# A hybrid GLA and attention trunk on one core: output-pair weight sums held behind low parts, products with g_post deferred, and loads moved ahead in the last pair

## The chip, the cores and the metric

The kernel runs on one NeuronCore of a Trainium2 chip. The metric is the device time of one execution in microseconds (us); lower is better. TensorE (PE) does the matrix products, with its weight loads shown as PEld; VectorE (DVE) and ScalarE (ACT) do elementwise work; GpSimd (POOL) issues some of the DMAs and does small powers; SyncE (SP) issues most DMAs. Each engine takes its instructions in the order of its own queue.

## The reference, cut to what matters

Two layers, 512 tokens, width 2048, float32. `w_in` has 7184 columns per layer, `w_out` 2048.

```python
def rmsnorm(x, g):
    y = xf * lax.rsqrt(jnp.mean(xf * xf, axis=-1, keepdims=True) + EPS) * g
def hybrid_layer(x, w_in, w_out, g_pre, g_post, ...):
    h = rmsnorm(x, g_pre)
    z = h @ w_in
    ...                       # gated linear attention, chunked attention, gates
    y = jnp.concatenate([o_gla, o_att], axis=-1) @ w_out
    return x + rmsnorm(y, g_post)
```

The change lies in the output projection `y = ... @ w_out`, its norm with `g_post` and the residual sum.

## The kernel before, in words

**Products.** Each float32 product is made of three matmuls in a rounded format (fp32r): the weight is split into a high part `wh` (a cast on ScalarE, L195) and a low part `wl` (source less high part, on VectorE, L203), the other operand likewise, and high·high, high·low and low·high are added up in PSUM. `w` lies in blocks of 512 columns, cut in 8 chunks of 256 rows; a chunk of one block is a tile of 128x1024 (512 KB).

**Jobs.** All weight tiles of the whole program form one list, `stream`, of objects `Job`. A job has three steps. `load` issues its DMAs on SP; `high` makes the sum or difference of weights that it needs (L189, L191 on VectorE) and then the cast; `low` makes the low part. The function `ahead` prepares, while job i is multiplied, loads up to five, `high` up to four and `low` up to three jobs in front. A job is 12 matmuls of 128x512.

**Two kinds of product.** `std_gemm` multiplies block by block. `fast_gemm` multiplies a pair of blocks as a 2x2 block product with seven products instead of eight (Winograd's form of Strassen): the kinds are P1 to P7, each with four chunks c, so 28 jobs. P5, P6 and (in the output pairs) P4 add a freshly loaded weight tile `r` to the running tile `H`; P7 takes a difference. The order of a pair is written out: `PROD_OUT` for the first output pair (W01), `PROD_END` for the second (W23) of the last layer:

```python
PROD_END = order("10 20 11 21 12 22 13 23 50 51 60 52 61 53 62 63 30 31 32 33 70 71 72 73 40 41 42 43")
PROD_OUT = order("10 20 11 21 12 13 50 51 60 61 22 23 52 53 62 63 30 31 32 33 70 71 72 73 40 41 42 43")
```

("51" is P5 with c = 1.) W23 of the first layer goes through `std_gemm`.

**Operands of the output pairs.** P1, P2 and P4 use the operands themselves (`og`, `op_att`: tiles `a` and `g`); P5, P6, P3 and P7 use their sums S1, S2, S4, S3. `output_sums` makes these during W01 on VectorE (L1157, then the low part L106) and ScalarE, each queued behind the latest low part of a weight. In the last layer they also go to DRAM (`so_d`, tile `oS`), and W23 loads them back as `sa`, a ring of four tiles.

**Rings.** `H` has four tiles, `raw` five, `wh` four, `wl` three, `sa` four; a load waits on SP until a tile of its ring is free.

**After a product.** `finished` hands each half result to `project`: its square sum on ScalarE (L1301), then the product with `g_post` on VectorE (L1304) into `ys`. Where the result is still to be combined (`combine`, L341), it goes to a scratch tile `t2` first. `finish_token` later scales with the norm and adds the residual. In W23 of the last layer the residual of the last 256 tokens is loaded by `Tokens.load` (L452), one or two of its six pieces after each job of P7; P7's own weight tiles are loaded into spare slots `g` at P3's load.

**Order.** The program text only gives dependencies and priorities: a planner puts each engine's instructions in an order by a simulated timeline. `tc.issue_after(x)` adds one edge: what is traced inside it stands behind x in its engine's queue, not necessarily right behind it. Side work runs as generators in `tasks`, stepped by `pump` from a `Pace` of so many steps per job.

Of the kernel before, what the change touches and what calls it, by code (L numbers as in the profile page):

```python
# [15 lines left out]
P = 128  # L16
# [17 lines left out]
def hybrid_trunk(  # L34
# [30 lines left out]
    def nm(s):  # L65
        serial[0] += 1
        return f"{s}_{serial[0]}"
# [65 lines left out]
    PROD_OUT = order("10 20 11 21 12 13 50 51 60 61 22 23 52 53 62 63 30 31 32 33 70 71 72 73 40 41 42 43")  # L133
    LEFT = {"P5": "S1", "P6": "S2", "P3": "S4", "P7": "S3", "P4": "A22"}
    SPARE = ("g12", "g13", "g16", "g17")
    last_cast, last_low, last_mm, last_load = [None], [None], [None], [None]

    class Job:
        def __init__(self, l, kind, c, b0, b1=None, pair=None):
# [13 lines left out]
        def load(self):  # L153
            k, c, p, b0, b1 = self.kind, self.c, self.pair, self.b0, self.b1
            end = b0 >= NB_IN and k != "std"
            if end:
                c = OC[c]
            top, bottom = (c + 4, c) if end else (c, c + 4)
            if k == "std":
                self.raw = self.fetch(rtile("raw", bufs=5), b0, c)  # L160
            elif k == "P1":
                p["H", self.c] = self.fetch(rtile("H"), b0, top)
            elif k == "P5":
                p["r", self.c] = self.fetch(rtile("raw", bufs=5), b1, top)
            elif k == "P6":
                p["r", self.c] = self.fetch(rtile("raw", bufs=5), b1, bottom)
            elif k == "P7":
                p["r", self.c] = p.pop(("t", self.c)) if b0 == W23[0] else self.fetch(rtile("raw", bufs=5), b0, top)
            elif k == "P2" or (k == "P4" and end):
                p["r", self.c] = self.fetch(rtile("raw", bufs=5), b0, bottom)  # L170
            sums = so_d if end else sa_d[self.l]
            src = sums.get((LEFT.get(k), c))
            if src is not None and b0 != NB_IN and not (k == "P5" and b0 == AV0):
                until(lambda: k == "P4" or (id(sums), LEFT[k], c) in written)
                self.a = rtile("sa", (2, 512), F32R)
                last_load[0] = nc.sync.dma_start(flat(self.a), src).ins
            if k == "P3" and b0 == W23[0]:
                with tc.issue_after(last_load[0]):
                    p["t", self.c] = self.fetch(slot(SPARE[self.c], [2, 512]), b0, c + 4)

        def high(self):
            k, c, p = self.kind, self.c, self.pair
            if k == "std":
                src = self.raw
            else:
                h, r = p["H", c], p.get(("r", c))
                src = h if k in ("P1", "P5", "P6", "P4") else r
                if k in ("P5", "P6") or (k == "P4" and self.b0 >= NB_IN):
                    nc.vector.tensor_tensor(out=h, in0=h, in1=r, op=ALU.add)  # L189
                elif k == "P7":  # L190
                    nc.vector.tensor_tensor(out=r, in0=h, in1=r, op=ALU.subtract)  # L191
            self.src = src
            self.wh = rtile("wh", dtype=F32R)
            for z in self.parts():
                last_cast[0] = nc.scalar.copy(self.wh[:, z, :], src[:, z, :]).ins  # L195
# [4 lines left out]
        def low(self):  # L200
            self.wl = rtile("wl", dtype=F32R, bufs=3)
            for z in self.parts():
                last_low[0] = nc.vector.tensor_tensor(  # L203
                    out=self.wl[:, z, :], in0=self.src[:, z, :], in1=self.wh[:, z, :].bitcast(F32), op=ALU.subtract
                ).ins
            if self.kind == "P2" and self.b0 < NB_IN:
                h = self.pair["H", self.c]
                nc.vector.tensor_tensor(out=h, in0=h, in1=self.src, op=ALU.add)  # L208
# [237 lines left out]
    XS1 = ("g9", "g10")  # L446

    class Tokens(list):
        def load(self, n=None):
            for z, src in self.moves[:n]:  # L450
                with tc.issue_after(last_load[0]):
                    nc.sync.dma_start(z, src)  # L452
            del self.moves[:n]

# [249 lines left out]
    def layer(l):  # L704
# [476 lines left out]
        def turn_gla(h, p):  # L1181
            ps = aux()
            for f in range(2):
                for tt in range(2):
                    nc.tensor.transpose(
                        ps[:, f * 256 + tt * P : f * 256 + (tt + 1) * P],
                        normed[h, p][:, tt, f * P : (f + 1) * P], ident,
                    )
            assert p or h >= 2 or ("P2", h) in passed
            op = slot(OG[p, h], [2, 512], F32R)  # L1190
            full_o = out_parts(h)[2 * p + 1]
            for f in range(2):
# [8 lines left out]
            if len(og) == 8:  # L1201
                for n in range(2):
                    gains.append(tmp.tile([P, W], F32, tag="bias", name=nm("bias"), bufs=2))
                    load_gain(n, gains[n])

        def gla_heads(j, gvh, gvl):
            units = []
# [83 lines left out]
            nc.sync.dma_start(gp, bass.AP(tensor=src.tensor, offset=src.offset, ap=[[0, P], [1, W]]))  # L1291
            return gp

        def project(o, n, src, gp, between=None):
            if o not in ssy:
                ssy[o] = sm(5, "ssy", 4)
                nc.gpsimd.memset(ssy[o][:, 4:5], EPS)
            if (o, n // 2) not in ys:
                ys[o, n // 2] = slot(YS[n // 2][o], [1024])
            j = t2(dtype=BF16)  # L1300
            nc.scalar.activation(j, src, AF.Square, scale=D ** -0.5, accum_out=ssy[o][:, n : n + 1])  # L1301
            if between is not None:
                between()
            nc.vector.tensor_tensor(  # L1304
                out=ys[o, n // 2][:, (n % 2) * W : (n % 2 + 1) * W], in0=src, in1=gp, op=ALU.mult
            )

        def out_evac(n):
            gp = load_gain(n, t2())
# [42 lines left out]
        def out_consume(n):  # L1352
            if n:
                gains[:] = [load_gain(n + j, t2()) for j in range(2)]
            ends = []

            def f(j, h, t, src, comb):
                until(lambda: len(gains) == 2)
                o = 2 * h + t
                ending = last and n == 2 and (j, h) == (0, 1)  # L1360

                def begin():
                    ends.append(finish_token(o, xs[1][t]))
                    next(ends[-1])

                with nullcontext() if n and (j, h) == (0, 1) else tc.issue_after(last_low[0]):
                    project(o, n + j, src if comb is None else comb(t2()), gains[j], begin if ending else None)
# [12 lines left out]
        drain()  # L1380

        def residual(k, c):
            if (k, c) == ("P3", 3):
                xs[1] = load_tokens(1, x_src)
            elif k == "P7":
                xs[1].load(2 if c > 1 else 1)

        if last:
            fast_gemm(
                l, W23, out_consume(2), rate=3, end=True, lag=2, ops=O,  # L1390
                after=residual,
            )
        else:
            for half in range(2):
                for b in W23:
                    if b == W23[1]:
                        xs[half] = load_tokens(half, x_src)
                        xs[half].load()
# [65 lines left out]
```

## Time and profile before

| | |
|---|---|
| median of 3 runs | 1643.17 us (1640.9 to 1645.68) |
| the profiled execution's own time | 1639.9 us |
| its span in the profile | 1637.8 us |
| mean granted TensorE clock | 0.997 |
| TensorE busy | 1613.9 us (99%) |
| VectorE busy | 1253.2 us (77%) |
| ScalarE busy | 911.4 us (56%) |
| HBM read, written | 371.25 MB, 55.33 MB |

Times in the rows of the trace count from the start of the span. In a timeline a row gives the start, the duration, engine, line, operation, `out<-in` by the program's names, shapes and count; in brackets stand the idle time of the engine before it and what ended it. A window row gives, behind the stretch and its length, the busy time of PE, PEld, DVE, ACT and POOL with the number of instructions, then the granted TensorE clock, the busy share of the DMA engines and GB/s. The matmuls are pipelined, so the duration of one (about 0.39 us) is longer than the distance from start to start.

### The profile page before, as it was taken

What the parts mean: (1) busy time and instruction counts of PE and PEld (TensorE: products, weight loads), DVE (VectorE), ACT (ScalarE), POOL (GpSimd) and SP (SyncE); (2) the same over time, 40 slices, a digit from 0 to 9 for tenths busy, and PEclk for the clock granted to TensorE, in tenths of its full rate; (3) what the DMA queues carried; (4) which work ended last, traced back from release to release, by engine and by line L of the source; (5) the groups of instructions that cost most, each with busy time, mean ns of one, the idle gap of its engine ahead of it and who ended that gap; (6) DMA issues with size and microseconds to landing.
All of it is one profiled execution on the core that took longest, in us unless ns stands there. A gap on an engine that the chain in (4) does not pass through costs nothing.

```text
span 1637.8 us, 24501 instructions
## 1 busy us (share of the span) xinstructions
PE 1613.9 (99%) x8986; PEld 1382.4 (84%) x8986; DVE 1253.2 (77%) x1630; ACT 911.4 (56%) x1497; POOL 122.0 (7%) x182
## 2 busy tenths in 40 slices
PE   9999999999999999999999999999999999999996
PEld 7888999998888778788788889999988887787885
DVE  5987778687787868995786667776776878699976
ACT  7554445666554556654674444455665545566553
POOL 0120000100000100000122000000000101101001
PEclk9999999999999999999999999999999999999999
DMA  9698685785869667277989486858858596785967
GB/s 368 239 377 283 229 308 196 251 305 173 297 201 354 223 220 262 95 262 267 332 278 398 172 309 220 305 184 271 272 175 296 186 333 232 232 297 200 347 232 228
DMA packets 130759, 426.10 MB, mean 260 GB/s; under 512 B 14052, under 2 KB 26852, under 8 KB 130608
## 3 DMA queue, kind: packets, MB, share of 16 engines
q1 hardware_dynamic: 115632, 370.22, 65.2%
q0 software_dynamic: 14432, 53.24, 8.8%
q8 instruction: 71, 1.16, 0.3%
q10 hardware_dynamic: 576, 1.08, 0.2%
q14 instruction: 48, 0.39, 0.1%
HBM read 371.25 MB, written 55.33 MB: 260 GB/s over the span
## 4 chain that ended last, share of the span: by engine, by line
PE 89%; DVE 5%; DMA 4%; issue 1%; ACT 1%; DVEq 0%; POOL 0%; SPq 0%; ACTq 0%; POOLq 0%
PE mm L384 46%; PE mm L374 19%; PE mm L306 12%; PE ax L907 2%; DVE wl L203 1%; PE ax L384 1%; PE ax L1092 1%; DMA H<-in_w_dram 1%; PE ax L890 1%; DMA raw<-in_w_dram 1%; DMA x_mid<-g 1%; PE ax L1064 1%; DVE g L106 1%; PE ax L871 1%; PE ax L870 1%
## 5 line engine op out<-in xcount | busy, mean ns | idle before, releaser
L384 PE MATMUL mm<-wh,sa 128*128 128x512 f32 x1472 | 479.1, 395 | 6.4 <-DMA sa<-oS 4.8
L195 ACT CAST wh<-raw 128x1024 fp32r<-128x1024 f32 (+1 forms) x249 | 261.3, 1053 | 223.1 <-PE mm L384 88.1
L203 DVE TENSOR_TENSOR wl<-raw,wh 128x1024 fp32r<-128x1024 f32 (+1 forms) x249 | 302.5, 1218 | 92.2 <-PE mm L384 31.6
L195 ACT CAST wh<-H 128x1024 fp32r<-128x1024 f32 x240 | 251.6, 1051 | 212.2 <-PE mm L384 96.8
L203 DVE TENSOR_TENSOR wl<-H,wh 128x1024 fp32r<-128x1024 f32 x240 | 292.9, 1222 | 91.8 <-PE mm L384 34.4
L384 PEld LDWEIGHTS mm<-wh,sa 128*128 128x128 f32 x1472 | 276.5, 188 | 74.1 <-issue 11.7
L384 PE MATMUL mm<-wl,sa 128*128 128x512 f32 x736 | 288.9, 392 | 4.3 <-DVE wl L203 4.3
L374 PE MATMUL mm<-sa,wh 128*128 128x256 f32 x1280 | 236.8, 285 | 0.0
L384 PE MATMUL mm<-wh,a 128*128 128x512 f32 x608 | 200.5, 394 | 0.5 <-ACT wh L195 0.5
L374 PEld LDWEIGHTS mm<-sa,wh 128*128 128x128 f32 x1280 | 200.0, 191 | 0.3
L374 PE MATMUL mm<-sa,wl 128*128 128x256 f32 x640 | 181.1, 283 | 0.0
L189 DVE TENSOR_TENSOR H<-H,raw 128x1024 f32<-128x1024 f32 x132 | 160.3, 1221 | 7.9 <-DMA raw<-in_w_dram 6.6
L384 PEld LDWEIGHTS mm<-wl,sa 128*128 128x128 f32 x736 | 138.7, 188 | 32.5 <-DVE wl L203 5.4
L384 PEld LDWEIGHTS mm<-wh,a 128*128 128x128 f32 x608 | 113.5, 188 | 24.4 <-ACT wh L195 0.9
L374 PEld LDWEIGHTS mm<-sa,wl 128*128 128x128 f32 x640 | 122.5, 191 | 0.0
L425 POOL TENSOR_TENSOR sm<-sm,mhalf 128x2 f32<-128x2 f32 (+2 forms) x42 | 52.8, 1258 | 934.3 <-DVE sm L917 452.5
L384 PE MATMUL mm<-wl,a 128*128 128x512 f32 x304 | 119.8, 394 | 0.0
L191 DVE TENSOR_TENSOR raw<-H,raw 128x1024 f32<-128x1024 f32 x56 | 68.6, 1225 | 45.2 <-DMA raw<-in_w_dram 45.0
L374 PE MATMUL mm<-a,wh 128*128 128x256 f32 x512 | 95.3, 285 | 0.0
L306 PE MATMUL mm<-wh,a 128*128 128x512 f32 x288 | 91.5, 390 | 0.0
L384 PE MATMUL mm<-wh,g 128*128 128x512 f32 x288 | 90.9, 390 | 0.2 <-ACT wh L195 0.2
L208 DVE TENSOR_TENSOR H<-H,raw 128x1024 f32<-128x1024 f32 x48 | 58.7, 1224 | 33.2 <-DMA raw<-in_w_dram 33.2
(235 smaller groups left out, 2429.3 us busy)
## 6 DMA issues: line engine op xcount, KB each, us to landing
raw<-in_w_dram SPq DMA_DIRECT2D x319, 512.0 KB, 4.9
sa<-S SPq DMA_DIRECT2D x184, 512.0 KB, 4.4
H<-in_w_dram SPq DMA_DIRECT2D x60, 512.0 KB, 5.1
sa<-A SPq DMA_DIRECT2D x48, 512.0 KB, 6.1
S<-g POOLq DMA_DIRECT2D x32, 512.0 KB, 8.9
sa<-oS SPq DMA_DIRECT2D x16, 512.0 KB, 5.9
oa<-g POOLq DMA_DIRECT2D x12, 512.0 KB, 6.4
g<-in_x_dram SPq DMA_DIRECT2D x10, 512.0 KB, 9.1
```

Of the source, the lines that this page charges most:

```text
L106: return nc.vector.tensor_tensor(out=lo, in0=src, in1=hi.bitcast(F32), op=ALU.subtract).ins
L189: nc.vector.tensor_tensor(out=h, in0=h, in1=r, op=ALU.add)
L191: nc.vector.tensor_tensor(out=r, in0=h, in1=r, op=ALU.subtract)
L195: last_cast[0] = nc.scalar.copy(self.wh[:, z, :], src[:, z, :]).ins
L203: last_low[0] = nc.vector.tensor_tensor(out=self.wl[:, z, :], in0=self.src[:, z, :], in1=self.wh[:, z, :].bitcast(F32), op=ALU.subtract).ins
L208: nc.vector.tensor_tensor(out=h, in0=h, in1=self.src, op=ALU.add)
L306: nc.tensor.matmul(pss[o], a(part, kk, o) if callable(a) else a[:, part, t], rhs[:, kk, :], start=(i == 0 and kk == 0 and m == 0), stop=(i ...
L374: nc.tensor.matmul(dst, lhs[:, kk, f], a[:, part, tok], start=(fresh and kk == 0 and m == 0 and ft % 2 == 0), stop=(c == 3 and kk == 1 and ...
L384: last_mm[0] = nc.tensor.matmul(out_ps[t], a[:, part, tok], rhs[:, kk, :], start=(fresh and kk == 0 and m == 0), stop=(c == 3 and kk == 1 ...
L425: nc.gpsimd.tensor_tensor(out=out_r, in0=v, in1=mhalf[:, : v.shape[-1]], op=ALU.pow)
L870: nc.tensor.matmul(ps[:, :n], self.qh[:, t], self.kl[:, :n], start=False, stop=False)
L907: nc.tensor.matmul(o, self.pt[i][:, j * P : (j + 1) * P], av[hd // 4, j // 2][:, j % 2, (hd % 4) * P : (hd % 4 + 1) * P], start=(j == 0), ...
```

## The change

Three edits. In the output pairs, `high` traces its addition or subtraction of weights inside `issue_after(lows[-2])`, where `lows` lists the low parts of all jobs. W01's results are no longer multiplied with `g_post` where they are evicted: `project` leaves the plain result in `ys`, and a generator `late_gains` multiplies the eight halves in place during W23. In W23 of the last layer the residual's six pieces are loaded one at a time behind `last_h`, the load of P1's last `H`, and P7's weight tiles are fetched at P5's load, also behind it.

```diff
+    lows = []
...
             elif k == "P1":
                 p["H", self.c] = self.fetch(rtile("H"), b0, top)
+                last_h[0] = last_load[0]
...
-            if k == "P3" and b0 == W23[0]:
-                with tc.issue_after(last_load[0]):
+            if k == "P5" and b0 == W23[0]:
+                with tc.issue_after(last_h[0]):
                     p["t", self.c] = self.fetch(slot(SPARE[self.c], [2, 512]), b0, c + 4)
...
-                if k in ("P5", "P6") or (k == "P4" and self.b0 >= NB_IN):
-                    nc.vector.tensor_tensor(out=h, in0=h, in1=r, op=ALU.add)
-                elif k == "P7":
-                    nc.vector.tensor_tensor(out=r, in0=h, in1=r, op=ALU.subtract)
+                with tc.issue_after(lows[-2]) if self.b0 >= NB_IN else nullcontext():
+                    if k in ("P5", "P6") or (k == "P4" and self.b0 >= NB_IN):
+                        nc.vector.tensor_tensor(out=h, in0=h, in1=r, op=ALU.add)
+                    elif k == "P7":
+                        nc.vector.tensor_tensor(out=r, in0=h, in1=r, op=ALU.subtract)
...
+            lows.append(last_low[0])
...
-        def project(o, n, src, gp, between=None):
+        def project(o, n, src, gp=None, comb=None, between=None):
...
+            dst = ys[o, n // 2][:, (n % 2) * W : (n % 2 + 1) * W]
+            y = src if comb is None else comb(dst if gp is None else t2())
+            if gp is None and comb is None:
+                nc.scalar.copy(dst, src)
...
-            nc.vector.tensor_tensor(
-                out=ys[o, n // 2][:, (n % 2) * W : (n % 2 + 1) * W], in0=src, in1=gp, op=ALU.mult
-            )
+            if gp is not None:
+                nc.vector.tensor_tensor(out=dst, in0=y, in1=gp, op=ALU.mult)
+
+        def late_gains():
+            gs = [load_gain(n, t2()) for n in range(2)]
+            for o in range(NT):
+                for n in range(2):
+                    for _ in range(3):
+                        yield
+                    dst = ys[o, 0][:, n * W : (n + 1) * W]
+                    with tc.issue_after(last_low[0]):
+                        nc.vector.tensor_tensor(out=dst, in0=dst, in1=gs[n], op=ALU.mult)
...
         drain()
+        tasks.append(late_gains())
 
         def residual(k, c):
-            if (k, c) == ("P3", 3):
+            if (k, c) == ("P2", 0):
                 xs[1] = load_tokens(1, x_src)
-            elif k == "P7":
-                xs[1].load(2 if c > 1 else 1)
+            if k in ("P1", "P2") and xs:
+                xs[1].load(last_h[0], 1)
```

More of the change, by code (lines that the diff above doesn't have):

```diff
@@ L135, in hybrid_trunk @@
     SPARE = ("g12", "g13", "g16", "g17")
-    last_cast, last_low, last_mm, last_load = [None], [None], [None], [None]
+    lows = []
+    last_cast, last_low, last_mm, last_load, last_h = [None], [None], [None], [None], [None]
     class Job:
@@ L448, in hybrid_trunk, with load @@
     class Tokens(list):
-        def load(self, n=None):
+        def load(self, behind, n=None):
             for z, src in self.moves[:n]:
-                with tc.issue_after(last_load[0]):
+                with tc.issue_after(behind):
                     nc.sync.dma_start(z, src)
@@ L1200, in turn_gla @@
             O[1, p, OC.index(h)] = op
[L1201 to L1204, printed above, removed]
         def gla_heads(j, gvh, gvl):
@@ L1299, in project @@
                 ys[o, n // 2] = slot(YS[n // 2][o], [1024])
+            dst = ys[o, n // 2][:, (n % 2) * W : (n % 2 + 1) * W]
+            y = src if comb is None else comb(dst if gp is None else t2())
+            if gp is None and comb is None:
+                nc.scalar.copy(dst, src)
             j = t2(dtype=BF16)
-            nc.scalar.activation(j, src, AF.Square, scale=D ** -0.5, accum_out=ssy[o][:, n : n + 1])
+            nc.scalar.activation(j, y, AF.Square, scale=D ** -0.5, accum_out=ssy[o][:, n : n + 1])
             if between is not None:
                 between()
-            nc.vector.tensor_tensor(
-                out=ys[o, n // 2][:, (n % 2) * W : (n % 2 + 1) * W], in0=src, in1=gp, op=ALU.mult
-            )
+            if gp is not None:
[9 more added lines that the diff above has]
+                        nc.vector.tensor_tensor(out=dst, in0=dst, in1=gs[n], op=ALU.mult)
         def out_evac(n):
@@ L1357, in f @@
             def f(j, h, t, src, comb):
-                until(lambda: len(gains) == 2)
                 o = 2 * h + t
@@ L1366, in f @@
                 with nullcontext() if n and (j, h) == (0, 1) else tc.issue_after(last_low[0]):
-                    project(o, n + j, src if comb is None else comb(t2()), gains[j], begin if ending else None)
+                    project(o, n + j, src, gains[j] if n else None, comb, begin if ending else None)
                 if last and n == 2 and (j, h, t) == (1, 0, 1):
@@ L1397, in layer @@
                         xs[half] = load_tokens(half, x_src)
-                        xs[half].load()
+                        xs[half].load(last_load[0])
                     std_gemm(l, b, (2 * half, 2 * half + 1), OL, operand_out, out_evac(b - NB_IN), rate=3, lag=2)
```

## The prediction

> **What bounds the kernel now.** I began with the page's engine totals.
>
> ```profile
> span 1637.8 us, 24501 instructions
> PE 1613.9 (99%) x8986; PEld 1382.4 (84%) x8986; DVE 1253.2 (77%) x1630; ACT 911.4 (56%) x1497; POOL 122.0 (7%) x182
> ```
>
> TensorE sets the time: 1613.9 of 1637.8 us busy. The diff touches no matmul, so it can gain only what TensorE idles, or runs at a lower clock, in the output pairs (W01 of both layers, W23 of the last). I therefore took a table of windows over the span and went into those where PE falls short.
>
> ```profile
> core 0: us, PE busy (x) PEld busy (x) DVE busy (x) ACT busy (x) POOL busy (x), PEclk, DMA share, GB/s
> 688.00:692.00 4.00, 1.95 (x7) 1.35 (x8) 4.00 (x5) 3.79 (x6) 0.00 (x0) 1.00 0.00 0
> 1508.00:1510.00 2.00, 2.00 (x6) 1.60 (x5) 2.00 (x3) 2.00 (x5) 0.00 (x0) 0.50 0.21 84
> 1510.00:1512.00 2.00, 2.00 (x8) 1.56 (x7) 2.00 (x4) 1.45 (x4) 0.00 (x0) 0.73 0.00 0
> 1565.00:1570.00 5.00, 5.00 (x24) 4.14 (x23) 4.22 (x4) 3.04 (x4) 0.00 (x0) 1.00 0.35 107
> 1600.00:1605.00 5.00, 3.00 (x12) 2.18 (x12) 2.06 (x3) 0.26 (x1) 0.00 (x0) 1.00 1.04 400
> ```
>
> There are three holes: W01 of layer 0 (about 690) and of layer 1 (before 1508, seen by the clock of 0.50 behind it), both with VectorE full, and W23 of layer 1 (1600) with the DMA engines full, although 35 us earlier, at 1565, they were busy for 0.35 only. The timeline of PE gives their sizes.
>
> ```profile
> 686.69 0.39 PE L384 MATMUL mm<-wh,sa 128*128 128x512 f32 x1
> 688.44 0.73 PE L384 MATMUL mm<-wh,sa 128*128 128x512 f32 x2 [1.36 <-ACT wh L195]
> 690.78 0.50 PE L384 MATMUL mm<-wl,sa 128*128 128x512 f32 x1 [1.61 <-DVE wl L203]
> 1503.11 0.40 PE L384 MATMUL mm<-wh,sa 128*128 128x512 f32 x1
> 1503.80 0.73 PE L384 MATMUL mm<-wh,sa 128*128 128x512 f32 x2 [0.30 <-ACT wh L195]
> 1507.26 0.50 PE L384 MATMUL mm<-wl,sa 128*128 128x512 f32 x1 [2.72 <-DVE wl L203]
> 1598.07 0.39 PE L384 MATMUL mm<-wh,sa 128*128 128x512 f32 x1
> 1601.66 0.47 PE L384 MATMUL mm<-wh,sa 128*128 128x512 f32 x1 [3.20 <-DMA sa<-oS]
> 1604.05 0.39 PE L384 MATMUL mm<-wl,sa 128*128 128x512 f32 x1
> 1604.27 0.39 PE L384 MATMUL mm<-wh,sa 128*128 128x512 f32 x1
> 1606.25 0.47 PE L384 MATMUL mm<-wh,sa 128*128 128x512 f32 x1 [1.59 <-DMA sa<-oS]
> ```
>
> Matmuls in step start 0.22 to 0.23 us apart (1604.05, 1604.27), so a job of 12 takes 2.7 us, and a hole is the next start less the last start less 0.23 per matmul. Layer 0: 688.44 − 686.92 = 1.52 and 690.78 − 688.90 = 1.88, together **3.40 us**. Layer 1: 0.46 + 3.00 = **3.46 us**. W23: 3.36 + 1.75 = **5.11 us**. Behind the layer-1 hole the granted clock halves: 2.0 us at 0.50 and 2.0 us at 0.73, which lose 1.0 and 0.5, **1.5 us**. All that can be won is 3.40 + 3.46 + 1.5 + 5.11 = 13.5 us, 0.8% of the time.
>
> **The change part by part.** *(a) VectorE's order in the output pairs.* Each add or subtract of weights (L189, L191) is now held behind the low part (L203) of the job two in front. What stood ahead of the late low parts (689.50 and 1505.97, both of P6's third job):
>
> ```profile
> 661.51 1.23 DVE L189 TENSOR_TENSOR H<-H,raw 128x1024 f32<-128x1024 f32 x1 [2.52 <-DMA raw<-in_w_dram]
> 662.65 1.22 DVE L203 TENSOR_TENSOR wl<-H,wh 128x1024 fp32r<-128x1024 f32 x1
> 684.29 1.22 DVE L191 TENSOR_TENSOR raw<-H,raw 128x1024 f32<-128x1024 f32 x1
> 685.43 0.69 DVE L106 TENSOR_TENSOR sa<-t,sa 128x512 fp32r<-128x512 f32 x1
> 689.50 1.23 DVE L203 TENSOR_TENSOR wl<-H,wh 128x1024 fp32r<-128x1024 f32 x1
> 1479.24 2.36 DVE L189 TENSOR_TENSOR H<-H,raw 128x1024 f32<-128x1024 f32 x2 [2.44 <-DMA raw<-in_w_dram]
> 1502.50 1.23 DVE L191 TENSOR_TENSOR raw<-H,raw 128x1024 f32<-128x1024 f32 x1
> 1505.97 1.23 DVE L203 TENSOR_TENSOR wl<-H,wh 128x1024 fp32r<-128x1024 f32 x1
> L195 ACT CAST wh<-H 128x1024 fp32r<-128x1024 f32 x240 | 251.6, 1051 | 212.2 <-PE mm L384 96.8
> ```
>
> An instruction of 128x1024 holds the queue for 685.43 − 684.29 = 1.14 us. L191 at 684.29 (1502.50) is P7's first subtract, six jobs ahead of its turn: P6's third job is the 15th of the pair, P7's first the 21st. Held behind the low part of the 19th, it leaves the way: 1.14 us in each layer. The add at 661.51 is P6's first; it made VectorE idle 2.52 us for its load while a ready low part (662.65, P5's first) stood behind it. Now that low part goes ahead and fills 1.14 us of the idle time; layer 1 has the same picture at 1479.24 (2.44 us). So 2 × 1.14 = **2.3 us** of each hole goes, and 1.1 us stays. Bounds: nothing (the planner orders other work into the place) to the whole 3.40 and 3.46. I take 2.3, the two named rows. With a hole of 1.1 us I let the clock's 1.5 us go as well, because layer 0's holes of 1.52 and 1.88 us left the clock at 1.00 (688 to 692). Sum of (a): 2.3 + 2.3 + 1.5 = **6.1 us**, bounds 0 and 8.4. The hold puts an add behind a low part two jobs in front, which leaves it two jobs, 5.4 us, for add (1.2), cast (1.1, the L195 row) and low (1.2): nobody waits for that unless the low part itself is late.
>
> The Trainium skill, TensorE: Matmul & The Clock Gate, Part 1, says that the clock drops to half after an idle window of about 3.4 us, and that the window runs freely. Here a hole of 3.00 us (3.46 with the two matmuls in it) was followed by half speed and one of 3.36 us was not, so the trace agrees with the free window and not with a fixed limit of 3.4 us. By the limit alone the 1.5 us would not hang on this hole, and the sum below would be 9.7 us.
>
> *(b) The products with g_post.* W01 no longer multiplies on VectorE; what is late next there is VectorE again, for it stays nearly full behind the hole:
>
> ```profile
> 694.71 0.70 DVE L1304 TENSOR_TENSOR a<-t,bias 128x512 f32<-128x512 f32 x1
> 695.31 0.69 DVE L341 TENSOR_TENSOR t<-ax,ev 128x512 f32<-128x512 f32 x1
> 700.00:729.00 29.00, 29.00 (x130) 24.01 (x129) 27.82 (x31) 15.25 (x23) 0.00 (x0) 1.00 0.76 276
> 729.00:760.00 31.00, 31.00 (x138) 25.70 (x137) 17.29 (x16) 14.56 (x20) 0.00 (x0) 1.00 0.82 283
> 1544.00:1572.00 28.00, 28.00 (x125) 23.18 (x124) 23.26 (x23) 15.49 (x21) 0.00 (x0) 1.00 0.67 229
> ```
>
> A multiply holds the queue for 0.60 us; eight are 4.8 us per layer out of a stretch with 27.82 of 29 us busy. TensorE did not wait there, so this wins nothing by itself, but it pays for TensorE's coming 2.3 us earlier and for P7's subtract, which returns here (1.14). The eight come back in W23, one every three steps of the task list. In layer 0 they lie beside work with VectorE busy 17.29 of 31 us: nothing. In the last layer they fall on the first eight jobs (1544 to 1572), 23.26 of 28 us busy; early adds of P5 and P6 leave that stretch by (a). I take nothing; without cover it is 8 × 0.60 = 4.8 us, and I keep 0 to 4.8. Two copies per layer go to ScalarE (15.49 of 28 us busy) and two 256 KB loads of g_post move behind W01: nothing.
>
> *(c) The loads.* In W23 of the last layer six residual loads and four of P7 (each group 2.1 MB) move in front of P5.
>
> ```profile
> 1537.01 3.69 SPq L150 DMA_DIRECT2D H<-in_w_dram  x3
> 1546.93 16.68 SPq L150 DMA_DIRECT2D raw<-in_w_dram  x8
> 1546.62 0.61 PE L384 MATMUL mm<-wh,a 128*128 128x512 f32 x2
> 1597.75 0.32 SPq L176 DMA_DIRECT2D sa<-oS  x1
> raw<-in_w_dram SPq DMA_DIRECT2D x8, 512.0 KB, 4.6
> sa<-oS SPq DMA_DIRECT2D x4, 512.0 KB, 9.4
> H<-in_w_dram SPq DMA_DIRECT2D x4, 512.0 KB, 9.4
> ```
>
> (The second-last column of the last three is KB, the last the median us to landing, from the DMA view of the windows 1546 to 1566, 1585 to 1600 and 1534 to 1541.) At 400 GB/s 4.2 MB are 10.5 us. They were issued in the stage of P3 and P7, where the operand sums (sa) among them took 9.4 us to land against the 4.6 us of the raw loads 35 us earlier; both waits of W23 are on sa. A slot of sa (four of them) frees four jobs, 10.9 us, ahead of use, so at 5 us both waits go: **5.1 us**, bounds 0 and 5.1. Ahead, the ten go behind P1's last H (issued by 1540.7, landed 9.4 us later, about 1550) and end about 1561. What is late next: the raw load of 1546.93, P5's second. Its job is the tenth of W23, whose first matmul is that of 1546.62, so it is due at 1546.6 + 9 × 2.72 = 1571, less 3.5 us for add, cast and low; it lands about 1563, 4 us early.
>
> Sum: 6.1 + 5.1 = **11.2 us**. The profiled execution took 1639.9 us (its span and 2.1 us around it) and would take 1628.7; it lies 3.3 us (0.2%) under the median of the three runs, 1643.17. On the median: **1632.0 us**.
>
> **The rivals.**
> 1. *Only the loads help.* VectorE's holes stay, because the sums of the output pair (L106, L1157), which the change leaves, close up to the late low part. For it: they stand in that queue too (685.43 is one). 1643.2 − 5.1 = 1638.1.
> 2. *Only VectorE's order helps.* "Behind" is a bound on one side: the planner may put the ten loads anywhere later on SP, also where they were. Against it: the raw loads of P5 stand at 1546.93 in the trace, 24 us ahead of their jobs, so the planner issues a load as soon as it may. 1643.2 − 6.1 = 1637.1.
> 3. *Neither does what it says*: 1643.2.
> 4. *Slower: the ring of raw turns too slowly in W23.* By (a) the adds run later, so raw's five slots come free later, while the ten loads crowd the same queue. A load that takes a freed slot is due five jobs on: 5 × 2.72 − 3.5 = 10.1 us. At 4.6 us to landing this never shows, at the crowd's 9.4 us just not. With the ten loads in front (10.5 us) it is 10.5 + 4.6 = 15.1 us, 5.0 us late per turn of the ring, and the twelve jobs of P5, P6 and P4 are 2.4 turns: 12 us lost. It decides from 10.1 us to landing. Then 12.0 − 6.1 = 5.9 slower: 1649.1. Against it: the crowd lasts 10.5 us, one turn and not 2.4. The Trainium skill, DMA: Bandwidth & Descriptors, Issuing engines are not separate DMA queues, says that all transfers interleave on the same 16 engines; by it the ten take their time from the H and raw loads beside them, which speaks for this rival.
>
> **How the numbers follow.** Forecast 0.50, rival 1 0.12, rival 2 0.13, rival 3 0.08, rival 4 0.17. About 0.3% (4.9 us) is what a measurement of this kernel can tell from no change. Rival 1 lies on that edge and is split; of rival 2 a little falls within. Faster 0.50 + 0.06 + 0.10 = 0.66; within 0.3% 0.06 + 0.03 + 0.08 = 0.17; slower 0.17. The range goes from all holes closed less part of the runs' spread, 1643.2 − 13.5 − 2.5 = 1627, to rival 3 and its spread, 1645; it leaves out rival 4 alone. The faster cases' own range is 1627 to 1639.
>
> **What would show it.** In the profile after: the holes near 687 and 1503 at 1.1 us or less, no half clock behind 1507, P7's first subtract behind the low part of P3's third job; no multiply on VectorE in W01 and eight of 0.69 us in W23; g and x_mid loads on SP right behind the last H, and no wait of PE for sa<-oS. The prediction is wrong if W23 waits for raw or H, if a hole of over 2.5 us stays in W01, or if an idle time of TensorE appears where there was none.

## The result and the profile after

The changed kernel took **1628.57 us** (median of 4 runs, 1627.89 to 1629.86) against 1642.04 us of the kernel before in the same set (4 runs, 1640.45 to 1645.68): 13.5 us less, ratio 0.9916 [0.9903, 0.9929]. The profiled execution took 1629.86 us with a span of 1627.8 us, 10.0 us less than before. Why the two differences differ is told at the end. Two executions of the kernel before beside experiments 1 to 4 took 2285 and 3256 us, far from all others, and are left out of every comparison. Lines have moved by 3 to 5: matmul L388, cast L198, low part L206, add L192, subtract L194, product with g_post L1309 and, deferred, L1319.

The page of the profile after begins so:

```profile
span 1627.8 us, 24499 instructions
PE 1612.6 (99%) x8986; PEld 1381.1 (85%) x8986; DVE 1251.5 (77%) x1630; ACT 911.3 (56%) x1501; POOL 121.9 (7%) x182
```

The work is what it was; the idle time is not. Next the view that sums up what PE waited for (us in total, times, longest), all of it from 0.3 us on:

```profile
PE ax L911 <- ACT t L897: 1.4, 1, 1.4
PE mm L388 <- ACT wh L198: 1.2, 3, 0.6
PE ax L661 <- DVE t L658: 1.2, 1, 1.2
PE mm L388 <- DVE wl L206: 0.8, 2, 0.5
PE ax L501 <- DVE g L491: 0.8, 1, 0.8
```

No wait for `sa` is left. Before, the same view gave 4.8 us for `sa<-oS`, 4.3 for the low part and 2.4 for the cast. The timeline of PE shows the two places of W01 and three that are new in W23:

```profile
686.39 0.84 PE L388 MATMUL mm<-wh,sa 128*128 128x512 f32 x3
687.62 0.50 PE L388 MATMUL mm<-wl,sa 128*128 128x512 f32 x1 [0.39 <-DVE wl L206]
...
1497.58 0.84 PE L388 MATMUL mm<-wh,sa 128*128 128x512 f32 x3
1498.68 0.72 PE L388 MATMUL mm<-wh,sa 128*128 128x512 f32 x2 [0.26 <-ACT wh L198]
...
1567.56 0.73 PE L388 MATMUL mm<-wh,sa 128*128 128x512 f32 x2 [0.38 <-ACT wh L198]
...
1571.16 0.74 PE L388 MATMUL mm<-wh,sa 128*128 128x512 f32 x2 [0.58 <-ACT wh L198]
...
1575.21 0.50 PE L388 MATMUL mm<-wl,sa 128*128 128x512 f32 x1 [0.45 <-DVE wl L206]
```

W01's holes are now 687.62 − 686.39 − 3 × 0.23 = 0.54 and 1498.68 − 1497.58 − 0.69 = 0.41 us. Among W23's P5 and P6 jobs (called P5's stage below) there are 0.55, 0.74 and 0.61 us, together 1.9, where there was nothing. From here on holes are counted with each matmul's own start less 0.227 us; the kernel before then has 3.30 and 3.36 us in W01, where the prediction counted 3.40 and 3.46, and 5.11 us in W23.

The windows after (columns as in the prediction) have no half clock behind W01's hole of layer 1, and TensorE busy throughout where `sa` was late:

```profile
1498.00:1505.00 7.00, 6.74 (x29) 5.05 (x28) 6.36 (x8) 4.47 (x6) 0.53 (x1) 1.00 0.71 274
...
1600.00:1605.00 5.00, 5.00 (x24) 4.14 (x23) 5.00 (x8) 4.02 (x6) 2.71 (x3) 1.00 0.00 0
```

VectorE's timeline shows P6's first add without the 2.5 us of idle time, P7's first subtract behind the low part of P3's third job (694.50), and the source of the new holes: five deferred products in a bunch in front of P5's second add.

```profile
659.49 1.22 DVE L206 TENSOR_TENSOR wl<-H,wh 128x1024 fp32r<-128x1024 f32 x1
660.75 1.22 DVE L192 TENSOR_TENSOR H<-H,raw 128x1024 f32<-128x1024 f32 x1
...
694.50 1.21 DVE L206 TENSOR_TENSOR wl<-raw,wh 128x1024 fp32r<-128x1024 f32 x1
...
696.84 1.21 DVE L194 TENSOR_TENSOR raw<-H,raw 128x1024 f32<-128x1024 f32 x1
...
1555.71 1.22 DVE L206 TENSOR_TENSOR wl<-H,wh 128x1024 fp32r<-128x1024 f32 x1 [1.51 <-PE ax L388]
1556.85 1.28 DVE L1319 TENSOR_TENSOR a<-a,t 128x512 f32<-128x512 f32 x2
1558.06 0.68 DVE L1319 TENSOR_TENSOR g<-g,t 128x512 f32<-128x512 f32 x1
1558.66 1.28 DVE L1319 TENSOR_TENSOR a<-a,t 128x512 f32<-128x512 f32 x2
1559.86 1.22 DVE L192 TENSOR_TENSOR H<-H,raw 128x1024 f32<-128x1024 f32 x1
```

SP's queue has the residual's loads (L456) right behind the load of P1's last `H`:

```profile
1534.50 0.33 SPq L151 DMA_DIRECT2D H<-in_w_dram  x1
1534.88 1.25 SPq L456 DMA_DIRECT2D g<-x_mid  x2
```

The DMA views of 1549 to 1562 and of 1585 to 1600 (KB, median us to landing) show the raw loads behind the moved ones, and the sums no longer crowded:

```profile
raw<-in_w_dram SPq DMA_DIRECT2D x6, 512.0 KB, 7.1
sa<-oS SPq DMA_DIRECT2D x5, 512.0 KB, 3.4
```

So the 10.0 us of the two spans are: W01 3.30 + 3.36 − 0.55 − 0.42 = 5.7, its half clock 1.7, W23 5.11 − 1.9 = 3.2, less about 0.5 us for waits of other stages (the one at L911 grew by 0.9 us, the one at L501 fell by 0.4): 10.1.

### The profile page after: what moved, and what is told of

Same layout as the page of the kernel before. It is cut to its first block, busy times and chain, and to the rows that moved or that the text cites. A ratio compares the mean times of both kernels' runs of the same rounds, so it can differ in the third digit from the quotient of the medians.

```text
span 1627.8 us, 24499 instructions
## 1 busy us (share of the span) xinstructions
PE 1612.6 (99%) x8986; PEld 1381.1 (85%) x8986; DVE 1251.5 (77%) x1630; ACT 911.3 (56%) x1501; POOL 121.9 (7%) x182
## 3 DMA queue, kind: packets, MB, share of 16 engines
q8 instruction: 71, 1.16, 0.3%
q10 hardware_dynamic: 576, 1.08, 0.2%
## 4 chain that ended last, share of the span: by engine, by line
PE 93%; DVE 3%; DMA 2%; issue 1%; ACT 1%; SPq 0%; POOL 0%; DVEq 0%; ACTq 0%; POOLq 0%
PE mm L388 48%; PE mm L378 19%; PE mm L310 14%; PE ax L911 2%; PE ax L388 1%; PE ax L1096 1%; PE ax L894 1%; PE ax L731 1%; PE ax L1068 1%; DMA x_mid<-g 1%; DVE wl L206 1%; PE ax L875 1%; PE ax L874 1%; PE ax L873 1%; DVE H L192 1%
## 5 line engine op out<-in xcount | busy, mean ns | idle before, releaser
L388 PE MATMUL mm<-wh,sa 128*128 128x512 f32 x1472 | 478.1, 395 | 1.2 <-ACT wh L198 1.2
L198 ACT CAST wh<-raw 128x1024 fp32r<-128x1024 f32 (+1 forms) x249 | 261.2, 1053 | 230.8 <-PE mm L388 88.5
L206 DVE TENSOR_TENSOR wl<-raw,wh 128x1024 fp32r<-128x1024 f32 (+1 forms) x249 | 301.7, 1215 | 89.5 <-PE mm L388 35.4
L206 DVE TENSOR_TENSOR wl<-H,wh 128x1024 fp32r<-128x1024 f32 x240 | 292.3, 1219 | 97.1 <-PE mm L388 32.8
L198 ACT CAST wh<-H 128x1024 fp32r<-128x1024 f32 x240 | 251.7, 1051 | 197.1 <-PE mm L388 86.4
L388 PEld LDWEIGHTS mm<-wh,sa 128*128 128x128 f32 x1472 | 275.4, 188 | 68.8 <-issue 8.5
L388 PE MATMUL mm<-wl,sa 128*128 128x512 f32 x736 | 288.1, 391 | 0.8 <-DVE wl L206 0.8
L388 PE MATMUL mm<-wh,a 128*128 128x512 f32 x608 | 200.9, 394 | 0.0
L388 PEld LDWEIGHTS mm<-wl,sa 128*128 128x128 f32 x736 | 138.3, 188 | 28.7 <-DVE wl L206 1.7
L192 DVE TENSOR_TENSOR H<-H,raw 128x1024 f32<-128x1024 f32 x132 | 160.1, 1217 | 1.2
L388 PEld LDWEIGHTS mm<-wh,a 128*128 128x128 f32 x608 | 113.5, 188 | 23.6
L388 PE MATMUL mm<-wl,a 128*128 128x512 f32 x304 | 119.6, 393 | 0.0
L194 DVE TENSOR_TENSOR raw<-H,raw 128x1024 f32<-128x1024 f32 x56 | 68.4, 1222 | 46.4 <-DMA raw<-in_w_dram 46.2
L388 PE MATMUL mm<-wh,g 128*128 128x512 f32 x288 | 90.9, 389 | 0.0
L340 ACT COPY ev<-mm 128x512 f32<-128x512 f32 x96 | 56.1, 584 | 57.4 <-PE mm L388 40.9
```

The costliest lines, as they stand in the source:

```text
L206: last_low[0] = nc.vector.tensor_tensor(out=self.wl[:, z, :], in0=self.src[:, z, :], in1=self.wh[:, z, :].bitcast(F32), op=ALU.subtract).ins
L340: nc.scalar.copy(e, src[t])
L388: last_mm[0] = nc.tensor.matmul(out_ps[t], a[:, part, tok], rhs[:, kk, :], start=(fresh and kk == 0 and m == 0), stop=(c == 3 and kk == 1 ...
```

## The experiments

All are measured beside the kernel before. The three parts of the change are called the hold (adds and subtracts of weights kept behind a low part), the deferral (the products with `g_post` made late) and the loads. The last two columns are the holes over 0.35 us in each profiled execution; in W01, neighbouring ones in one place are added up. Line numbers differ by up to 5 between these kernels: an add is `H<-H,raw`, a subtract `raw<-H,raw` or `g<-H,g`, a low part `wl<-`.

| | time, us | ratio to before, 95% interval | W01, layers 0 and 1 | W23 |
|---|---|---|---|---|
| before | 1640.7 to 1642.0 | 1 | 3.30, 3.36 | 3.36 + 1.75 |
| changed | 1628.57 | 0.9916 [0.9903, 0.9929] | 0.55, 0.42 | 0.55 + 0.74 + 0.61 |
| 1 hold only | 1635.01 | 0.9962 [0.9949, 0.9975] | 0.56, 0.44 | 2.21 + 3.06 |
| 2 deferral only | 1637.81 | 0.9981 [0.9968, 0.9993] | 1.80, 1.69 | 0.38 + 2.49 + 1.48 |
| 3 loads only | 1639.11 | 0.9983 [0.9970, 0.9995] | 3.31, 3.39 | 2.27 |
| 4 hold and loads | 1628.18 | 0.9925 [0.9907, 0.9942] | 0.56, 0.43 | none |
| 5 g_post on GpSimd's queue | 1637.49 | 0.9979 [0.9970, 0.9988] | 1.80, 2.33 + 0.48 | 3.13 + 0.59 |
| 6 hold of P7 only | 1639.47 | 0.9991 [0.9979, 1.0002] | 2.17 + 0.39, 2.12 | 2.21 + 3.04 |
| 7 products in P3's stage | 1632.56 | 0.9947 [0.9933, 0.9961] | 0.56, 0.43 | 3.99 |
| 8 changed again | 1629.26 | 0.9933 [0.9917, 0.9950] | 0.56, 0.43 | 0.54 + 0.75 + 0.61 |
| 9 hold in W01 only | 1633.24 | 0.9956 [0.9943, 0.9968] | 0.56, 0.43 | 0.55 + 1.69 + 0.36 + 0.47 + 1.12 + 1.08 |
| 10 P7's loads as before | 1628.64 | 0.9923 [0.9909, 0.9936] | 0.56, 0.44 | 0.55 |
| 11 late g_post on GpSimd | 1628.41 | 0.9920 [0.9907, 0.9934] | 0.56, 0.43 | 0.56 + 0.60 |
| 12 hold and loads again | 1627.76 | 0.9917 [0.9903, 0.9930] | 0.56, 0.44 | none |

**1. The hold alone.** The kernel before with this part of the change, and nothing else:

```diff
+                with tc.issue_after(lows[-2]) if self.b0 >= NB_IN else nullcontext():
                     if k in ("P5", "P6") or (k == "P4" and self.b0 >= NB_IN):
...
+            lows.append(last_low[0])
```

> The kernel before with one edit: the adds and subtracts of weights in the output pairs stand behind the low part of the job two in front. Theory A (the order of VectorE's queue makes the holes of W01): both holes of W01 shrink from 3.40 and 3.46 us to about 1 us, the half clock behind 1507 goes, the two waits for sa in W23 (5.1 us) stay; 6 to 7 us faster than before (ratio 0.996). Theory B (VectorE has too much work in W01, and the eight products fewer are what closes the holes): the holes stay above 2.5 us, gain 0 to 2 us (ratio 0.999 to 1.000).

Both holes of W01 close to 0.56 and 0.44 us, not to 1.1, while W23's waits stay, by the view of PE's waits:

```profile
PE mm L387 <- DMA sa<-oS: 4.9, 2, 2.9
```

VectorE's order by itself is therefore worth more in W01 than I took, and nothing in W23's holes of before.

**2. The deferral alone.** The kernel before with the products moved, no hold, no moved loads:

```diff
-                    project(o, n + j, src if comb is None else comb(t2()), gains[j], begin if ending else None)
+                    project(o, n + j, src, gains[j] if n else None, comb, begin if ending else None)
...
+        tasks.append(late_gains())
```

> The kernel before with one edit: W01's products with g_post are left out at eviction and made in W23. Theory A: the holes of W01 keep their 3.4 us each, since the products stand behind them in the queue; W23's waits stay or grow by up to 2 us, because the late products come in a bunch; no gain, 0 to 3 us slower (ratio 1.000 to 1.002). Theory B: the holes of W01 go, 6 to 7 us faster (ratio 0.996).

Both theories missed: the holes halve, to 1.80 and 1.69 us. P7's early subtract is still ahead, so something else left. VectorE's timeline, this kernel:

```profile
659.05 1.23 DVE L191 TENSOR_TENSOR H<-H,raw 128x1024 f32<-128x1024 f32 x1 [0.78 <-DMA raw<-in_w_dram]
...
1474.84 1.23 DVE L191 TENSOR_TENSOR H<-H,raw 128x1024 f32<-128x1024 f32 x1 [0.77 <-DMA raw<-in_w_dram]
```

The idle time in front of the late add fell from 2.52 and 2.44 us to 0.78 and 0.77: the raw loads came earlier. SP's queue in the kernel before shows why:

```profile
1463.60 1.50 SPq L150 DMA_DIRECT2D raw<-in_w_dram  x2
1470.41 0.33 SPq L1291 DMA_DIRECT2D bias<-in_g_post_dram  x1
1470.84 0.85 SPq L150 DMA_DIRECT2D raw<-in_w_dram  x2
```

Between 1465 and 1470 SP issues nothing; then comes a g_post load into a tile `bias`, and two raw loads 0.4 us behind it. What SP's queue waited for between 1460 and 1480 names the cause:

```profile
SPq L1291 <- PE ax L1185: 9.5, 2, 5.0
```

The two g_post loads waited 9.5 us for matmuls that still read the old content of their tiles, and held what stood behind them. Experiment 5 tests what this costs.

**3. The loads alone.** The kernel before with the residual's and P7's loads moved:

```diff
-            if (k, c) == ("P3", 3):
+            if (k, c) == ("P2", 0):
                 xs[1] = load_tokens(1, x_src)
...
-            if k == "P3" and b0 == W23[0]:
-                with tc.issue_after(last_load[0]):
+            if k == "P5" and b0 == W23[0]:
+                with tc.issue_after(last_h[0]):
```

> The kernel before with one edit: the residual's six loads and P7's four go behind the load of P1's last H. Theory A: both waits of W23 for sa (5.1 us) go, W01 stays as before; 5 us faster (ratio 0.997), with no new wait in P5 of W23, as the late products are not there. Theory C (the loads need the products' deferral, because two of the residual's pieces lie in the tiles that hold g_post in W01, and wait for them at the head of SP's queue): the load of a raw tile for P5 comes late, a new hole of 2 us or more in P5 or P2 of W23, gain under 3 us (ratio above 0.998).

The waits for `sa` go, but a new one takes their place in W23's P6 stage, on the cast. PE and then VectorE:

```profile
1589.88 0.73 PE L387 MATMUL mm<-wh,sa 128*128 128x512 f32 x2 [2.11 <-ACT wh L197]
...
1587.04 1.22 DVE L193 TENSOR_TENSOR g<-H,g 128x1024 f32<-128x1024 f32 x1
1588.17 1.22 DVE L205 TENSOR_TENSOR wl<-H,wh 128x1024 fp32r<-128x1024 f32 x1
1589.31 1.23 DVE L193 TENSOR_TENSOR g<-H,g 128x1024 f32<-128x1024 f32 x1
```

P7's tiles are now there early, so the planner puts P7's subtracts (L193) between P6's adds and low parts. The early load gives W23 the trouble that W01 had. So theory A is right on the waits for `sa` and wrong on the gain, 2.8 us by the ratio and not 5; theory C has the size, but not the place, and no wait for the `bias` tiles.

**4. Hold and loads, no deferral.** The changed kernel with the products back at the eviction:

```diff
-        tasks.append(late_gains())
...
-                    project(o, n + j, src, gains[j] if n else None, comb, begin if ending else None)
+                    project(o, n + j, src, gains[j], comb, begin if ending else None)
```

> The changed kernel without its deferral: order of VectorE's queue and loads as in the change, products with g_post at eviction as before. Theory A: W01's holes at about 1 us or less, no wait for sa in W23, and the three new holes of 0.6 to 0.7 us at 1566 to 1575 gone, since no late products stand in front of P5's adds: as fast as the changed kernel or up to 2 us faster (ratio to before 0.990 to 0.992). Theory B: the holes of W01 come back at 2.5 us or more, 5 us slower than the changed kernel (ratio 0.995). Theory C: a hole of 2 us in W23 as with the loads alone (ratio 0.993).

1628.18 us, as the changed kernel, and W23 has no hole at all, as theory A said. With the hold in place the deferral adds nothing in W01 (0.56 and 0.43 us with it and without).

**5. The g_post loads on another queue.** The kernel before; products where they were:

```diff
-                    load_gain(n, gains[n])
+                    load_gain(n, gains[n], nc.gpsimd)
```

> The kernel before, with one edit: the two g_post loads of W01 in each layer are issued by GpSimd instead of SP; the products stay where they were. Theory Q (the deferral helped W01 because these two loads waited for their tile on SP and held the raw loads behind them): VectorE's idle time in front of the late add falls from about 2.5 us to under 1 us in both layers, and the holes of 3.40 and 3.46 us fall to about 1.8 and 1.7 us, as they did when the products were deferred alone (1.80 and 1.69); time 1637 to 1640 us. Theory V (it was the multiplications that VectorE no longer did in W01): the holes stay at 3.4 us and the time at 1642 us.

Theory Q holds in the main: 3.4 us less by the ratio, against 3.1 for the deferral alone (not all of it W01's: W23's waits are 1.4 us shorter in this profile). In layer 0 the hole is 1.80 us, as in experiment 2. In layer 1 it is 2.33, for some of VectorE's idle time (2.44 before) is left in front of the late add:

```profile
1476.71 2.36 DVE L189 TENSOR_TENSOR H<-H,raw 128x1024 f32<-128x1024 f32 x2 [1.15 <-DMA raw<-in_w_dram]
```

So what the deferral gave W01 came through SP's queue and not through VectorE's load: all of the 1.50 us in layer 0, and 1.03 of the 1.67 us in layer 1. Why layer 1 kept 1.15 us of idle time is open. The Trainium skill, DMA: Bandwidth & Descriptors, Issuing engines are not separate DMA queues, says that issuing from several engines saves only the sequencer's time, usually small. Here it went with 3.4 us, since what stood on SP was not the issuing but a wait for a tile.

**6. The hold for P7 alone.**

```diff
-                with tc.issue_after(lows[-2]) if self.b0 >= NB_IN else nullcontext():
+                with tc.issue_after(lows[-2]) if k == "P7" and self.b0 >= NB_IN else nullcontext():
```

> The kernel before, with the hold on P7's subtractions alone; the adds of P5, P6 and P4 are issued as before. Prediction's split: the early subtraction is 1.14 us of each hole, the load-blocked add the rest; the holes fall from 3.40 and 3.46 us to about 2.3 us each, and the time by 2 to 3 us (a half clock less behind one of them may add 1.5 us). Rival: the subtraction is all that the hold has to keep back, and the holes fall to 0.5 us as with the whole hold (0.56 and 0.44), time 1635 us. Other rival: the add is what counts and the holes stay above 2.8 us.

Holes of 2.17 and 2.12 us: 1.13 and 1.24 less than before. P7's early subtract is worth what the prediction gave it, 1.14; the held adds are worth the other 1.6 to 1.7. The time did not follow: the ratio 0.9991 [0.9979, 1.0002] is not clear of no change, where I expected 2 to 3 us. This profile has two stretches of 3.41 us at half speed behind its holes, the one before has one.

**7. The deferred products later, in P3's stage.**

```diff
+            for _ in range(42 if last else 0):
+                yield
             gs = [load_gain(n, t2()) for n in range(2)]
...
-                    for _ in range(3):
+                    for _ in range(2 if last else 3):
```

> The changed kernel, with the eight late products of the last layer begun later, in the stage of W23's P3 jobs (where VectorE has low parts alone), two steps apart instead of three. If the three new holes of W23's P5 stage (0.55, 0.74, 0.61 us, 1.9 us in all) come from the products that stand in a bunch in front of P5's additions: they go, no TensorE idle time over 0.3 us is new in P3's stage, and the time is 1 to 2 us under the changed kernel's. Rival: the holes stay, since the additions wait for something else (the raw loads behind the residual's on SP): time as the changed kernel's.

The three holes go, as the theory said, but the run is 3.3 us over the changed kernel beside it. POOL, ACT and PE, by the timeline:

```profile
1601.72 5.42 POOL L429 TENSOR_TENSOR sm<-sm,mhalf 128x1 f32<-128x1 f32 x1 [85.81 <-DVE sm L1334]
1607.17 1.15 ACT L1346 ACTIVATE a<-a,sm 128x1024 f32<-128x1024 f32 x1 [3.63 <-POOL sm L429]
1608.85 0.50 PE L388 MATMUL mm<-wh,g 128*128 128x512 f32 x1 [3.83 <-ACT ev L340]
```

The task list is worked in order, so the finishing of a token block came later too: its first scaling on ACT began at 1599.7 us in experiment 8 and at 1607.2 here. It waited for POOL, and the copy of a PSUM tile that TensorE needed stood behind it.

**8. The changed kernel again**, beside 5, 6 and 7.

> The changed kernel itself, beside the others of this set. Expected about 13.5 us under the kernel before (0.9916 of it), with holes of about 0.5 us in W01 and three of together 1.9 us in W23's P5 stage. If a half clock falls behind the layer boundary's or another remaining hole, its profiled span is longer by 1.7 us for each 3.4 us of it, with the same holes.

Same holes, to 0.01 us. Beside the kernel before it is 11.0 us faster by the ratio, not 13.5; the two intervals overlap. Its profiled span is 1625.3 us, 2.5 less than the first: the waits for L911 and L501 (1.4 and 0.8 us then) are not among its holes.

**9. The hold in W01 only.**

```diff
-                with tc.issue_after(lows[-2]) if self.b0 >= NB_IN else nullcontext():
+                with tc.issue_after(lows[-2]) if self.b0 == NB_IN else nullcontext():
```

> The changed kernel with the hold in W01 alone; in W23 adds and subtractions are issued without it, as before. Theory (the early loads of P7's weights need the hold, since without it VectorE is given P7's subtractions ahead of P6's additions): W01's holes stay near 0.5 us, and a hole of about 2.3 us appears in W23's P6 stage near 1580 us, as with the loads moved alone; the three holes of P5's stage may stay; time 1631 to 1634 us, 2 to 4 us over the changed kernel. Rival (the hold matters in W01 only, and the parts merely overlap in the measurement): no such hole, time as the changed kernel's, 1629 us.

1633.24 us, 4.6 over experiment 10 beside it. W23 now waits for low parts, and more often than the once that I expected:

```profile
1567.74 0.80 PE L388 MATMUL mm<-wl,sa 128*128 128x512 f32 x1 [1.51 <-DVE wl L206]
1581.56 0.50 PE L388 MATMUL mm<-wl,sa 128*128 128x512 f32 x1 [0.96 <-DVE wl L206]
```

The moved loads pay in full only with the hold.

**10. The residual moved, P7's loads as before.**

```diff
-            if k == "P5" and b0 == W23[0]:
-                with tc.issue_after(last_h[0]):
+            if k == "P3" and b0 == W23[0]:
+                with tc.issue_after(last_load[0]):
```

> The changed kernel with P7's weight loads back behind the sa loads of P3's jobs, as before; the residual's loads stay early. Prediction's reading (it was the residual that stood in front of the sa loads of P7 and P4, beside P7's weights): if both are needed for the 5.1 us, one of the two waits, some 2 to 2.5 us, comes back in P7's stage near 1590 us and the time is 1631 to 1632 us. Rival: the residual alone made both waits, and no wait for sa comes back: time as the changed kernel's or less, since fewer loads then stand in front of g_post's.

One hole of 0.55 us for `sa` is left, so the residual's loads made nearly all of the 5.1 us (the rival of the expectation). And the three holes of P5's stage are gone. PE, then VectorE:

```profile
1594.12 0.47 PE L388 MATMUL mm<-wh,sa 128*128 128x512 f32 x1 [0.39 <-DMA sa<-oS]
1552.63 1.23 DVE L206 TENSOR_TENSOR wl<-raw,wh 128x1024 fp32r<-128x1024 f32 x1 [0.36 <-issue]
1553.77 2.49 DVE L1319 TENSOR_TENSOR a<-a,t 128x512 f32<-128x512 f32 x4
1556.18 1.22 DVE L206 TENSOR_TENSOR wl<-H,wh 128x1024 fp32r<-128x1024 f32 x1
```

Four products stand in front of P5's first low part here, where the changed kernel's VectorE idled 1.51 us (its row at 1555.71), and the fifth behind it; the adds follow earlier.

**11. The late g_post loads on GpSimd's queue.**

```diff
-            gs = [load_gain(n, t2()) for n in range(2)]
+            gs = [load_gain(n, t2(), nc.gpsimd) for n in range(2)]
```

> The changed kernel with g_post's loads for the late products issued by GpSimd instead of SP. Theory (the products come in a bunch in P5's stage because their loads stand on SP behind the residual's and P7's weights, issued some 9 to 14 us behind the last H): the loads are issued 15 us earlier or more, the products are spread over P1's and P2's jobs, and the three holes of P5's stage (1.9 us) go; time 1626 to 1628 us, the lowest so far. Rival (the products themselves are too much for VectorE wherever they stand in W23): holes of together over 1 us stay, now in P1's or P2's stage; time as the changed kernel's, 1629 us.

My theory falls: the loads were issued 22 us earlier, but the products moved by no more than one add. GpSimd, then VectorE:

```profile
1522.54 1.16 POOL L1291 DMA_DIRECT2D t<-in_g_post_dram  x2 [6.50 <-ACT t L1305]
1555.95 1.22 DVE L192 TENSOR_TENSOR H<-H,raw 128x1024 f32<-128x1024 f32 x1
1557.09 1.29 DVE L1319 TENSOR_TENSOR a<-a,t 128x512 f32<-128x512 f32 x2
```

They stand at 1557.09, after P5's second add, because VectorE's order is written when the kernel is built and not when a load lands. Two of the three holes stay (1.16 us). With experiment 10 this points to the products' place in VectorE's order, against P5's adds and low parts, as what counts.

**12. Hold and loads again.**

> Hold and loads as changed, products at the eviction as before: the run of before once more, beside the others of this set. Expected 0.9925 of the kernel before as measured, with no hole over 0.4 us in W23; if deferring helps once its loads have a queue of their own, this run is about 1 us over that with the loads on GpSimd; if the late products only cost, it is the lower of the two.

1627.76 us, the lowest median, but 10 and 11 beside it lie within 0.9 us and their intervals overlap: no version is shown to beat the changed kernel.

## Why the prediction was right, and where it was not

The direction and the mechanism were right: forecast 11.2 us, spans 10.0, medians 13.5. That the sum came so near is partly luck: (a) was 1.1 us too small, and (b) put at nothing what cost 1.9. By its steps:

- **(a) VectorE's order, 2.3 us of each hole.** Measured about 2.75 and 2.94 (experiment 1 and the changed kernel). The first term, P7's subtract at 1.14, is confirmed (1.13 and 1.24, experiment 6). The second is the mis-sized one: I let the low part fill 1.14 us of the add's idle time, by one instruction. The changed kernel has no idle time there (660.75, no wait), and the term is 1.6 to 1.7.
- **The half clock, 1.5 us.** It left, worth half of 3.41 us, 1.7. The step let it go with a smaller hole, and it went. The reason given, that layer 0's holes of 1.52 and 1.88 us leave the clock at 1.00, holds for that one profile alone: experiment 3 has the same two holes and half speed behind them. Which holes cost it is told at the end.
- **(b) The products, 0 of 0 to 4.8 us.** The step that failed is the cover in the last layer. I put eight products beside a stretch with VectorE busy 23.26 of 28 us; that is a mean, and five of them stood in one bunch in front of an add. Cost 1.9 us. In W01 I saw the multiplies and not their two loads: the text moved "two 256 KB loads" at nothing, and with them out of SP's way W01's holes are 1.50 and 1.67 us smaller (experiment 2), or 1.50 and 1.03 (experiment 5). With the hold this adds nothing (experiment 4).
- **(c) The loads, 5.1 us.** Both waits went, `sa` landing in 3.4 us as against 9.4. But I summed (a) and (c) as if they were free of each other. Alone the loads gained 2.8 us, the hold 6.2, both 12.3 (by the ratios of experiments 3, 1 and 4, times 1641): the hold keeps P7's subtracts back in W23 once their tiles come early (experiments 3 and 9). The residual alone made 4.6 of the 5.1 (experiment 10).
- **The rivals.** Rival 1 (VectorE's holes stay) falls with experiment 1, which leaves 0.56 and 0.44 us of them. Rival 2 (the planner leaves the loads where they were) falls with SP's queue of the changed kernel, where the residual's first loads follow the last H at once (1534.88). Rival 4, the ring of raw, didn't show: its loads landed in 7.1 us, between the 4.6 of before and the 10.1 from which it decides, and PE waited for none. One sign that the prediction named for being wrong, idle time of TensorE where there was none, did appear, from the products: 1.9 us.

## What to carry to other kernels

On an engine that works in a fixed order, an operand that arrives earlier can make things worse, because the planner then puts its consumer in front of more urgent work (experiments 3 and 9); an early load needs a lower bound on its consumer's place. Count a DMA that is removed or moved by what stands behind it on its issuing queue, not by its bytes. Work moved "beside" an engine with room must be checked at its own place in the order, since a busy share over 28 us hides a bunch of 3 us.

## What the runs showed of the hardware

The granted clock's half-speed stretches lie on a grid. Where a profile has several, they begin a whole number of 3.413 us steps apart, and all but the one at the end, when TensorE is done, last one step (once two). I laid that grid over all fourteen profiles and took TensorE's idle time in each step outside the start and the tail. All nine steps with 2.11 us of idle time or more were followed by half speed, none of the 13 with 1.23 to 1.71 us was, and of four with 1.74 to 1.84 us two were. So in these 26 steps the limit is about half a step, and a hole's price hangs on where the grid cuts it. The kernel before shows it, then experiment 6, by windows laid on the grid, then experiment 3 behind its holes of layer 0:

```profile
1504.26:1507.67 3.41, 0.69 (x4) 0.37 (x3) 3.41 (x5) 1.98 (x3) 1.06 (x2) 1.00 0.62 244
1507.67:1511.08 3.41, 3.41 (x10) 2.64 (x9) 3.41 (x6) 2.86 (x6) 0.00 (x0) 0.50 0.22 90
1599.83:1603.24 3.41, 1.58 (x7) 1.34 (x8) 0.96 (x2) 0.00 (x0) 0.00 (x0) 1.00 1.03 396
```

```profile
1502.51:1505.92 3.41, 1.62 (x6) 0.76 (x5) 3.41 (x5) 3.11 (x5) 1.06 (x2) 1.00 0.95 380
1505.92:1509.33 3.41, 3.41 (x9) 2.65 (x9) 3.41 (x6) 2.69 (x5) 0.00 (x0) 0.50 0.30 119
```

```profile
691.00:694.00 3.00, 3.00 (x7) 2.42 (x8) 3.00 (x4) 2.48 (x5) 0.00 (x0) 0.50 0.00 0
```

The hole of 3.36 us was cut in two (1.83 us idle in one step) and cost no clock; one of 1.76 us in experiment 6, with a small one in the same step, did. The Trainium skill, TensorE: Matmul & The Clock Gate, Part 1, has the free-running window of 3413 ns, and the trace agrees; its condition, an idle window, is stricter than what these runs show.

The grid also explains the larger part of the 3.5 us between the two differences. Of these, 2.1 us are the kernel before, whose median lies that far above its profiled execution. Its holes in W01 and W23 can each be cut either way, 1.7 us a time: the profile before shows one half clock behind W01's holes, that of experiment 3, with the same holes, two. The mean granted clock of every execution is on record. Over the 55 of the kernel before beside the experiments it was 0.9952, and 0.9967 in the profiled one; 0.0015 of 1640 us are 2.5 us, an estimate of what the half clocks make. The 16 executions with 0.992 to 0.994 took 1642.7 us in the median, the ten with 0.997 or 0.998 took 1638.8. The other 1.3 us are the changed kernel, whose profiled execution was the slowest of its four, and this is not the clock, which was 0.999 there. Its waits for L911 and L501 are the likely cause, since the profile of experiment 8, without them, is 2.5 us shorter; this is argued, not shown.
